# Value products of a head in steps over the next head's jobs, four jobs between scores and transposes, and weight splits in quarters

## The chip, the cores and the metric

The kernel runs on one core of one Trainium2 chip. The metric is the device time of one execution in microseconds (us); lower is better. PE is TensorE (matmuls), DVE is VectorE, ACT is ScalarE, POOL is GpSimd, SP is SyncE, which issues most of the DMAs.

## What is computed

A network of two layers over 512 tokens: 256 context tokens and 256 latent tokens of width 1024. Each layer has a gated feed-forward part, then a mixer, then a second feed-forward part. Only the mixer concerns us. It projects the tokens, runs twelve attention heads and a state-space branch side by side, and puts the joined result through one output projection:

```python
def token_mixers(zx, zc, need_ctx_out, ...):
    a_x = na_attention(rms_norm(heads(qa_x), ...), rms_norm(heads(ka_x), ...), heads(va_x), ka_ch, va_ch, na_rpb)
    kb_c, vb_c = mla_keys_values(ckv_c, kr_c, ...)
    kb_x, vb_x = mla_keys_values(ckv_x, kr_x, ...)
    qb_x = rope_tail(mla_queries(cq_x, ...), row, col)
    kb_x = rope_tail(kb_x, row, col)
    b_x = blocked_joint_attention(qb_x, kb_x, vb_x, kb_c, vb_c, MLA_QK ** -0.5)
    s_x, s_c = s5_mixer(u_x, u_c, need_ctx_out, ...)
    ox = jnp.concatenate([a_x, b_x, s_x], axis=-1)
    if not need_ctx_out:
        return ox, None
    a_c = attend(...)
    b_c = attend(...)
    return ox, jnp.concatenate([a_c, b_c, s_c], axis=-1)
```

Heads 0 to 5 (`a`) are neighbourhood attention with a bias; heads 6 to 11 (`b`) are latent attention, whose queries, keys and values come from an up-projection of a narrow latent vector, with a norm and a rotation. Latent tokens attend to all 512 tokens, context tokens to the 256 context tokens. Context outputs are needed in layer 0 only (`need_ctx_out`). The state-space branch ends in a GELU and a gated linear unit (GLU). Softmax is over the keys, as usual: maximum, exponential, sum, division.

## The kernel before

Each layer's mixer ends in a stage that runs the twelve heads (`attention`). A head is cut into jobs: ("x", h, 0) and ("x", h, 1) for the two 128-row tiles of latent queries against 512 keys, and in layer 0 also ("c", h, 0) for both tiles of context queries, each against 256 keys. Layer 0 has 36 jobs, layer 1 has 24. In the profiled execution layer 0's stage lies at about 578 to 726 us, layer 1's at about 1677 to 1779 us.

The loop over jobs writes the order in which every engine takes its instructions; nothing reorders them at run time. In turn `i` it issues:

- the scores of job `i`: three matmuls on PE (L1522, context L1530; two more for the bias of heads 0 to 5, L1525) into one of four accumulator banks, the maximum on DVE (L1533, tile `m`), the exponential on ACT (L1537, tile `e`, its sum in `su`);
- the keys and queries of coming heads (`after`): copies that ACT and DVE share (L1444, L1445, L1454, L1455; for latent heads L1471, L1472, L1474, L1475);
- the scaling of job `i-1`: reciprocal on DVE (L1542) and a multiplication (L1544), on POOL for the first latent tile and for context, on DVE for the second latent tile;
- the transposes of job `i-LAG`, with LAG = 3: four on PE (L1553), copied out by DVE (L1559) or ACT (L1561) into `PTx` or `PTc`;
- the value products of a pair of heads, two turns after the pair's last transposes: 8 products for the latent rows or 4 for the context rows, in which the two heads take turns (L1571), then ACT and DVE evict both heads at once (L1574, L1575, into `xn`);
- one step of `latent()`: an up-projection for one token tile (L292 to L294), its norm and rotation, later the two halves of the GLU (L1360 to L1363), and at the end the split of the first output weight.

A weight is split into a rounded part and the rest: ACT copies halves (L252), DVE or POOL subtract (L253). PSUM banks: four accumulators (`acc`) for scores, and banks `t` and `b`, handed out by `tp()`, for transposes, value products, up-projections and the GLU. The output projection reads the planes of the mixer's output in the order `ks`. Bias for heads 0 to 5 is prepared on POOL (L1457 to L1460).

## Time and profile before

| | us |
|---|---|
| median of three runs | 2004.27 |
| lowest and highest | 2002.52 and 2012.45 |
| the profiled execution, its own time | 2008.59 |
| the profiled execution, span | 2006.8 |

Over the span PE is busy 95%, DVE 46%, ACT 34%, POOL 33%, and the mean granted clock of PE is 0.98 of full speed. An average over the span hides that the feed-forward parts and the two attention stages are different: the first keep PE busy without a break, the second don't. So the profile is read by stretches: how much of a stretch each engine works, who waits for whom in it, and then the timeline of the engine that waits. A timeline row gives the start, the duration, the engine, the line, the operation with its output and inputs, the count, and in brackets how long the engine stood idle before and what ended that.

### The profile page before, as it was taken

The numbers are of one execution on the slowest core, as the hardware profiler recorded it, in microseconds if no ns is written. First come the engines' busy times: TensorE is split into PE (matmuls) and PEld (weight loads), VectorE is DVE, ScalarE is ACT, GpSimd is POOL, SyncE is SP. The second block draws the span as 40 slices with busy tenths as digits, with TensorE's granted clock in tenths as the row PEclk, the third lists the DMA queues.
The fourth block names the chain that finished last, engine by engine and source line by source line (L and its number), as shares of the span: only waits on it lengthen the run. The fifth ranks groups of instructions, "written<-read, shape, count | busy, mean of one in ns | idle before, by whom it ended". The sixth has DMA issues, their size and how long they took to land. (4 is left out here: it accounts for less than half of the span.)

```text
span 2006.8 us, 28327 instructions
## 1 busy us (share of the span) xinstructions
PE 1904.8 (95%) x11435; PEld 1582.0 (79%) x11435; DVE 914.7 (46%) x1585; ACT 689.8 (34%) x1146; POOL 656.2 (33%) x739
## 2 busy tenths in 40 slices
PE   7999999999887799999999999999999998699999
PEld 4777777788886578788888877777788887579999
DVE  6443233255456545232332454422433645655555
ACT  4421222233345534222222342122122434545433
POOL 2146460134457443100101223845212445641000
PEclk9999999999989899999999999999999988999999
DMA  9655656444412014543322355646523451227653
GB/s 308 178 178 170 211 188 206 136 119 126 156 19 72 22 43 126 170 133 97 100 89 90 114 170 168 201 148 222 174 76 108 146 162 28 83 92 224 189 184 112
DMA packets 364102, 277.77 MB, mean 138 GB/s; under 512 B 29854, under 2 KB 355812, under 8 KB 363972
## 3 DMA queue, kind: packets, MB, share of 16 engines
q1 hardware_dynamic: 361008, 268.44, 43.5%
q0 software_dynamic: 1888, 7.31, 1.0%
q8 instruction: 90, 1.47, 0.3%
q10 hardware_dynamic: 1076, 0.22, 0.1%
...
## 5 line engine op out<-in xcount | busy, mean ns | idle before, releaser
L292 PE MATMUL acc<-xn,spl 128*128 128x512 f32 (+1 forms) x1648 | 591.3, 359 | 2.3 <-DVE xn L571 1.2
L293 PE MATMUL acc<-xn,spl 128*128 128x512 f32 (+1 forms) x1648 | 584.6, 355 | 1.9 <-DVE xn L398 0.2
L294 PE MATMUL acc<-xn,spl 128*128 128x512 f32 (+1 forms) x1648 | 580.9, 353 | 0.2 <-DVE spl L253 0.2
L253 DVE TENSOR_TENSOR spl<-raw,spl 128x1024 fp32r<-128x1024 f32 (+2 forms) x312 | 398.2, 1313 | 278.6 <-ACT spl L252 276.8
L252 ACT ACTIVATE spl<-raw 128x1024 fp32r<-128x1024 f32 (+3 forms) x344 | 324.0, 989 | 321.5 <-PE acc L294 164.9
L674 POOL TENSOR_TENSOR hid<-hv,hid 128x512 fp32r<-128x512 f32 (+1 forms) x88 | 101.8, 1156 | 854.0 <-ACT hid L673 854.0
L292 PEld LDWEIGHTS acc<-xn,spl 128*128 128x128 f32 x1648 | 311.7, 189 | 64.2 <-issue 17.8
L293 PEld LDWEIGHTS acc<-xn,spl 128*128 128x128 f32 x1648 | 311.8, 189 | 46.9 <-DVE xn L572 4.6
L294 PEld LDWEIGHTS acc<-xn,spl 128*128 128x128 f32 x1648 | 311.7, 189 | 44.1 <-DVE spl L253 0.9
L292 PE MATMUL acc<-hid,spl 128*128 128x512 f32 (+1 forms) x740 | 265.2, 358 | 0.0
L293 PE MATMUL acc<-hid,spl 128*128 128x512 f32 (+1 forms) x740 | 262.0, 354 | 0.0
L294 PE MATMUL acc<-hid,spl 128*128 128x512 f32 (+1 forms) x740 | 261.7, 354 | 0.0
L671 DVE TENSOR_TENSOR hv<-sl,acc 128x512 f32<-128x512 f32 (+1 forms) x88 | 54.6, 620 | 362.7 <-PE acc L294 350.7
L673 ACT ACTIVATE hid<-hv 128x512 fp32r<-128x512 f32 (+1 forms) x88 | 50.9, 579 | 383.2 <-DVE hv L671 383.2
L731 DVE SCALAR_TENSOR_TENSOR h<-acc,mod,h 128x256 f32<-128x256 f32 x192 | 84.9, 478 | 207.3 <-PE acc L294 207.3
L292 PEld LDWEIGHTS acc<-hid,spl 128*128 128x128 f32 x740 | 139.8, 189 | 25.2 <-issue 6.4
L294 PEld LDWEIGHTS acc<-hid,spl 128*128 128x128 f32 x740 | 139.9, 189 | 19.6
L293 PEld LDWEIGHTS acc<-hid,spl 128*128 128x128 f32 x740 | 140.0, 189 | 18.6
L293 PE MATMUL acc<-spl,xn 128*128 128x384 f32 (+1 forms) x288 | 98.0, 340 | 8.5 <-DVE spl L253 8.2
L292 PE MATMUL acc<-spl,xn 128*128 128x384 f32 (+1 forms) x288 | 101.2, 351 | 0.0
L294 PE MATMUL acc<-spl,xn 128*128 128x384 f32 (+1 forms) x288 | 97.5, 338 | 0.0
L669 ACT ACTIVATE sl<-acc 128x512 f32<-128x512 f32 (+1 forms) x88 | 47.7, 541 | 133.8 <-PE acc L294 127.5
...
## 6 DMA issues: line engine op xcount, KB each, us to landing
...
```

The source lines that it names most:

```text
L252: nc.scalar.activation(s[:, 0, a:b], raw[:, a:b], AF.Copy)
L253: (nc.gpsimd if mix and b == n else nc.vector).tensor_tensor(s[:, 1, a:b], raw[:, a:b], s[:, 0, a:b].bitcast(F32), op=OP.subtract)
L292: mm(out, sl[0], sr[0], start=start, stop=False)
L293: mm(out, sl[0], sr[1], start=False, stop=False)
L294: mm(out, sl[1], sr[0], start=False, stop=stop)
L669: nc.scalar.activation(sl[:, c], pg[:, c], AF.Silu)
L671: nc.vector.tensor_tensor(hv[:, c], sl[:, c], pu[:, c], op=OP.mult)
L673: nc.scalar.activation(hd[:, 0, c], hv[:, c], AF.Copy)
L674: nc.gpsimd.tensor_tensor(hd[:, 1, c], hv[:, c], hd[:, 0, c].bitcast(F32), op=OP.subtract)
L731: self.nc.vector.scalar_tensor_tensor(self.h[:, n, c], ps[:, c], self.mod[l][:, gate, n, s:s + 1], self.h[:, n, c], op0=OP.mult, op1=OP.add)
```

## The change

- The value products of one head become a generator (`pv`), in steps of one product. Two are issued per turn (`pvs(2)`), beginning one turn after the last transposes of the head, so they are spread over the jobs of the next head. Both heads of a pair share one bank `b`, which `tp()` doesn't hand out any more in this stage. An eviction follows the last product of the odd head, for latent and context rows each.
- LAG is 4; there are five buffers for `e` and `m`, six for `su`, two for `PTx` and `PTc`.
- The up-projections and the GLU take accumulators instead of `tp()` banks.
- The first step of `latent()` is issued before the first keys. The rotation of the shared key part goes one tile at a time into the first four steps.
- Weights are split in quarters (`parts`), one or two per step: ACT copies, DVE and POOL subtract in turn.
- The GLU (both halves in one step) and the split of the first output weight move into a new generator, `readout`, which takes the place of `latent` from job 19 in layer 0 and job 13 in layer 1.
- All scalings run on DVE but those of context rows of heads 6 to 11, which stay on POOL.
- Copies of transposes: DVE takes the second latent tile, ACT all others.
- The output projection reads the planes of heads 0 to 5 first, then the GLU's, then those of the latent heads.

```diff
--- before.py
+++ after.py
@@ -276,6 +276,22 @@
             j += 1
         if j < n:
             self.split(j)
+
+    def parts(self):
+
+        j = self.cur
+        if j in self.spl:
+            return []
+        nc, raw, n = self.nc, self.raws[j], self.width(j)
+        s = self.splp.tile([128, 2, 2048], F32R, name="spl", tag="spl")
+        self.spl[j] = s
+
+        def piece(i):
+            c = slice(i * n // 4, (i + 1) * n // 4)
+            nc.scalar.activation(s[:, 0, c], raw[:, c], AF.Copy)
+            (nc.vector, nc.gpsimd)[i % 2].tensor_tensor(s[:, 1, c], raw[:, c], s[:, 0, c].bitcast(F32), op=OP.subtract)
+
+        return [(lambda i=i: piece(i)) for i in range(4)]
 
     def fillers(self):
         while self.cur < len(self.units) and self.units[self.cur][0] == "mod":
@@ -1294,7 +1310,7 @@
         qs, kn, ss = {}, {}, {}
 
         def upproj(ct, w, nk, n, t):
-            ps = [self.tp(), self.tp()]
+            ps = [self.acc(), self.acc()]
             c = slice(128 * t, 128 * t + 128)
             for hf in range(2):
                 for k in range(nk):
@@ -1353,7 +1369,7 @@
 
             pg = {}
             for m in (2 + n, n):
-                pg[m] = self.tp()
+                pg[m] = self.acc()
                 for k in range(2):
                     self.mm3(pg[m][:, c], (wg[:, 0, k, m * 128:m * 128 + 128], wg[:, 1, k, m * 128:m * 128 + 128]), (yh[:, 0, k, c], yh[:, 1, k, c]), k == 0, k == 1)
             eg = mp2.tile([128, 576], F32, name="sq6")[:, 0:T]
@@ -1364,34 +1380,48 @@
 
         def latent():
 
-            w = self.take("uq", (l,))[:, :, 0:1728].rearrange("p s (k n) -> p s k n", k=3)
-            for t in (2, 3, 0, 1):
-                rope(kr[:, t].unsqueeze(1), t, 1, 1)
+            w = self.take("uq", (l,), False)[:, :, 0:1728].rearrange("p s (k n) -> p s k n", k=3)
+            parts = self.parts()
             seq = [(qhead, qstat, qtail, t) for t in [2, 3] + qt_[:-2]]
             nqs = len(seq)
             seq += [(khead, kstat, ktail, t) for t in al]
             for i in range(len(seq) + 2):
                 if i == nqs:
-                    w = self.take("ukv", (l,), True)[:, :, 0:1536].rearrange("p s (k n) -> p s k n", k=2)
+                    for f in parts:
+                        f()
+                    w = self.take("ukv", (l,), False)[:, :, 0:1536].rearrange("p s (k n) -> p s k n", k=2)
+                    parts = self.parts()
                 if i < len(seq):
                     seq[i][0](seq[i][3], w)
+                if i < 4:
+                    t = (2, 3, 0, 1)[i]
+                    rope(kr[:, t].unsqueeze(1), t, 1, 1)
                 for j in (1, 2):
                     if 0 <= i - j < len(seq):
                         seq[i - j][j](seq[i - j][3])
+                for f in parts[0:(1, 2)[i < nqs and nqs < 4]]:
+                    f()
+                    parts.remove(f)
                 yield
+            for f in parts:
+                f()
+
+        def readout():
             wg = self.take("glu", (l,), False)[:, :, 0:1024].rearrange("p s (k n) -> p s k n", k=2)
             for n in range(2):
                 glu(n, wg)
+            yield
+            for f in self.parts():
+                f()
                 yield
-            self.ahead()
-
-        self.attention(l, need, qt_, qk, nv, qs, kn, mv, biases, bias, xn, mp2, latent())
-
+
+        self.attention(l, need, qt_, qk, nv, qs, kn, mv, biases, bias, xn, mp2, latent(), readout())
         es.close()
+
         self.norm_open()
         self.sq_begin()
         halves = (0, 1) if need else (1,)
-        ks = [6, 7, 3, 4, 5, 0, 1, 2]
+        ks = [0, 1, 2, 6, 7, 3, 4, 5]
         for u in range(4):
             w = (early if u == 3 else self.take("out", (l, u))).rearrange("p s (k n) -> p s k n", k=8)
             ps = [self.acc(), self.acc()]
@@ -1418,7 +1448,7 @@
             for n in (2 * u, 2 * u + 1):
                 self.sq_tile(n, c)
 
-    def attention(self, l, need, qt_, qk, nv, qs, kn, mv, biases, bias, ox, ap, latent):
+    def attention(self, l, need, qt_, qk, nv, qs, kn, mv, biases, bias, ox, ap, latent, readout):
 
 
 
@@ -1529,10 +1559,10 @@
                     for i, (q, k) in enumerate(terms):
                         mm(s[:, 256 * b:256 * b + 256], q[:, 128 * b:128 * b + 128], k[:, 0:256], start=i == 0, stop=i == 2)
                 nb, n = 2, 256
-            m = ap.tile([128, 2], F32, name="m", bufs=4)
+            m = ap.tile([128, 2], F32, name="m", bufs=5)
             V.tensor_reduce(m[:, 0:nb], s.rearrange("p (b n) -> p b n", b=nb), axis=AX, op=OP.max, negate=True)
-            e = ap.tile([128, 512], F32, name="e", bufs=4)
-            su = ap.tile([128, 2], F32, name="su", bufs=4)
+            e = ap.tile([128, 512], F32, name="e", bufs=5)
+            su = ap.tile([128, 2], F32, name="su", bufs=6)
             for i in range(nb):
                 S.activation(e[:, i * n:i * n + n], s[:, i * n:i * n + n], AF.Exp, bias=m[:, i:i + 1], accum_out=su[:, i:i + 1])
             st[j] = (e, su, nb, n)
@@ -1541,13 +1571,13 @@
             e, su, nb, n = st[j]
             V.reciprocal(su[:, 0:nb], su[:, 0:nb])
             for i in range(nb):
-                (P if j[2] == 0 else V).tensor_scalar(e[:, i * n:i * n + n], e[:, i * n:i * n + n], su[:, i:i + 1], None, op0=OP.mult)
+                (P if j[0] == "c" and j[1] >= 6 else V).tensor_scalar(e[:, i * n:i * n + n], e[:, i * n:i * n + n], su[:, i:i + 1], None, op0=OP.mult)
 
         def transposes(j):
             kind, h, t = j
             e = st.pop(j)[0]
             if (kind, h) not in PT:
-                PT[kind, h] = ap.tile([128, 4 if kind == "x" else 2, 256], F32, name=f"PT{kind}", bufs=3)
+                PT[kind, h] = ap.tile([128, 4 if kind == "x" else 2, 256], F32, name=f"PT{kind}", bufs=2)
             p = self.tp()
             for i in range(4):
                 nc.tensor.transpose(p[:, 128 * i:128 * i + 128], e[:, 128 * i:128 * i + 128], self.ident)
@@ -1555,28 +1585,41 @@
                 d, v = PT[kind, h][:, :, 128 * t:128 * t + 128], p.rearrange("p (k q) -> p k q", k=4)
             else:
                 d, v = PT[kind, h].rearrange("p k (t q) -> p t k q", t=2), p.rearrange("p (t k q) -> p t k q", t=2, k=2)
-            if t or (kind == "c" and h % 2):
+            if t:
                 V.tensor_copy(d, v)
             else:
                 S.activation(d, v, AF.Copy)
-            if h % 2 and (t or kind == "c"):
-                pend.append((kind, h))
-
-        def pv(kind, h):
-            o = self.tp()
-            nk = 4 if kind == "x" else 2
-            pts = [PT.pop((kind, h - 1)), PT.pop((kind, h))]
-            for k in range(nk):
-                for i in range(2):
-                    mm(o[64 * i:64 * i + 64, 0:256], value(h - 1 + i)(k), pts[i][:, k, :], start=(k == 0), stop=(k == nk - 1))
-            c = slice(256, 512) if kind == "x" else slice(0, 256)
-            f = h // 2 + 2
-            S.activation(ox[:, 0, f, c], o[:, 0:256], AF.Copy)
-            V.tensor_tensor(ox[:, 1, f, c], o[:, 0:256], ox[:, 0, f, c].bitcast(F32), op=OP.subtract)
-
-        pend = []
-        LAG = 3
-        old = [[], []]
+            if kind == "c" or (t and not need):
+                pend.append(h)
+
+        def pv(h):
+
+            i, f = h % 2, h // 2 + 2
+            if i == 0:
+                outs[h] = self.pm.tile([128, 512], F32, name="b", tag="b")
+            o = outs[h - i]
+            for kind in ("x", "c") if need else ("x",):
+                pt = PT.pop((kind, h))
+                c = slice(256, 512) if kind == "x" else slice(0, 256)
+                nk = 4 if kind == "x" else 2
+                for k in range(nk):
+                    mm(o[64 * i:64 * i + 64, c], value(h)(k), pt[:, k, :], start=k == 0, stop=k == nk - 1)
+                    if i and k == nk - 1:
+                        S.activation(ox[:, 0, f, c], o[:, c], AF.Copy)
+                        V.tensor_tensor(ox[:, 1, f, c], o[:, c], ox[:, 0, f, c].bitcast(F32), op=OP.subtract)
+                    yield
+
+        def pvs(n):
+            while n and steps:
+                if next(steps[0], 0) == 0:
+                    steps.pop(0)
+                else:
+                    n -= 1
+
+        pend, steps, outs = [], [], {}
+        LAG = 4
+        self.bank = True
+        next(latent)
         keys(0)
         queries(0)
         queries(1)
@@ -1588,13 +1631,15 @@
                 scale(jobs[i - 1])
             if i >= LAG:
                 transposes(jobs[i - LAG])
-            for a in old.pop(0):
-                pv(*a)
-            old.append(pend[:])
+            pvs(2)
+            steps += [pv(h) for h in pend]
             pend.clear()
-            next(latent, None)
-        for a in old[0] + old[1]:
-            pv(*a)
+            next(latent if i < 6 * each + 1 else readout, None)
+        while steps:
+            pvs(1)
+        for _ in readout:
+            pass
+        self.bank = None
 
 
     def run(self):
```

On PE, in heads 9 and 10 of layer 0 (L1522, L1530 are scores, L1553 transposes, L1571 value products, a pair in turns; `mv` are the values of latent heads), before:

```order
L1522 MATMUL acc<-xn,qz_4762 128x512 x3
L1553 MATMUL t<-k,e 128x128 x4
L1522 MATMUL acc<-xn,qz_4762 128x512 x3
L1553 MATMUL t<-k,e 128x128 x4
L1530 MATMUL acc<-xn,qz_4762 128x256 x6
L1553 MATMUL t<-k,e 128x128 x4
L1522 MATMUL acc<-kt,qz_4763 128x512 x3
L1553 MATMUL b<-k,e 128x128 x4
L1571 MATMUL t<-PTx,mv 64x256 x8
L1522 MATMUL acc<-kt,qz_4763 128x512 x3
L1553 MATMUL t<-k,e 128x128 x4
L1571 MATMUL t<-PTc,mv 64x256 x4
L1530 MATMUL acc<-kt,qz_4763 128x256 x6
```

and now (L1552, L1560 are scores, L1583 transposes, L1606 value products):

```order
L1552 MATMUL acc<-xn,qz_4762 128x512 x3
L1583 MATMUL t<-k,e 128x128 x4
L1606 MATMUL b<-PTc,mv 64x256 x2
L1552 MATMUL acc<-xn,qz_4762 128x512 x3
L1583 MATMUL t<-k,e 128x128 x4
L1606 MATMUL b<-PTx,mv 64x256 x2
L1560 MATMUL acc<-xn,qz_4762 128x256 x6
L1583 MATMUL t<-k,e 128x128 x4
L1606 MATMUL b<-PTx,mv 64x256 x2
L1552 MATMUL acc<-kt,qz_4763 128x512 x3
L1583 MATMUL t<-k,e 128x128 x4
L1606 MATMUL b<-PTc,mv 64x256 x2
```

The two bursts of 8 and 4 are now groups of two behind the transposes of each job.

On DVE, in jobs 11 to 14 of layer 0, around the GLU (L1361, L1363) and the split (L253), before:

```order
L1575 TENSOR_TENSOR xn<-t,xn 128x256
L1361 SCALAR_TENSOR_TENSOR sq_5381<-b,smT_90,sq_5381 128x512
L1363 TENSOR_TENSOR xn<-sq_5381,xn 128x512
L1533 TENSOR_REDUCE m<-acc 128x2
L1455 TENSOR_TENSOR qz_4763<-t,qz_4763 64x512
L1542 RECIPROCAL su<-su 128x1
L1544 TENSOR_SCALAR e<-e,su 128x512
L1361 SCALAR_TENSOR_TENSOR sq_5434<-b,smT_90,sq_5434 128x512
L1533 TENSOR_REDUCE m<-acc 128x1
L1542 RECIPROCAL su<-su 128x2
L253 TENSOR_TENSOR spl<-raw,spl 128x1024
L1533 TENSOR_REDUCE m<-acc 128x1
```

and now, around job 20 (L1377, L1379 are the GLU, L1563 the maximum, L1574 the scale, L292 a quarter of the split):

```order
L1572 RECIPROCAL su<-su 128x1
L1574 TENSOR_SCALAR e<-e,su 128x512
L1377 SCALAR_TENSOR_TENSOR sq_5624<-acc,smT_90,sq_5624 128x512
L1379 TENSOR_TENSOR xn<-sq_5624,xn 128x512
L1377 SCALAR_TENSOR_TENSOR sq_5643<-acc,smT_90,sq_5643 128x512
L1563 TENSOR_REDUCE m<-acc 128x2
L1502 TENSOR_TENSOR qz_4762<-t,qz_4762 96x512
L1505 SCALAR_TENSOR_TENSOR xn<-t,kg_92,xn 96x512
L1572 RECIPROCAL su<-su 128x1
L1574 TENSOR_SCALAR e<-e,su 128x512
L1589 COPY PTx<-t 128x4x128
L292 TENSOR_TENSOR spl<-raw,spl 128x512
```

The GLU's operations stood one job apart, each ahead of a maximum; now three stand together, eight jobs later, and the split has smaller pieces.

On DVE, in a late pair of heads of layer 0 (L1575 evictions, L1533 maxima, L1559 copies of transposes), before:

```order
L1544 TENSOR_SCALAR e<-e,su 128x512
L1559 COPY PTc<-t 128x2x2x128
L1533 TENSOR_REDUCE m<-acc 128x1
L1542 RECIPROCAL su<-su 128x2
L1575 TENSOR_TENSOR xn<-t,xn 128x256
L1533 TENSOR_REDUCE m<-acc 128x1
L1542 RECIPROCAL su<-su 128x1
L1559 COPY PTx<-b 128x4x128
L1575 TENSOR_TENSOR xn<-t,xn 128x256
L1533 TENSOR_REDUCE m<-acc 128x2
L1472 TENSOR_TENSOR qz_4763<-t,qz_4763 96x512
```

and now (L1609 evictions, L1589 copies):

```order
L1572 RECIPROCAL su<-su 128x1
L1574 TENSOR_SCALAR e<-e,su 128x512
L1589 COPY PTx<-t 128x4x128
L1609 TENSOR_TENSOR xn<-b,xn 128x256
L1563 TENSOR_REDUCE m<-acc 128x1
L1572 RECIPROCAL su<-su 128x2
L1609 TENSOR_TENSOR xn<-b,xn 128x256
L1563 TENSOR_REDUCE m<-acc 128x1
L1572 RECIPROCAL su<-su 128x1
L1574 TENSOR_SCALAR e<-e,su 128x512
L1563 TENSOR_REDUCE m<-acc 128x2
```

Copies of context transposes have left DVE, scales of the first latent tile have come to it.

## Rows read from the trace of the kernel before

**Rows 1.** Busy time by stretch: length; busy (count) PE, PEld, DVE, ACT, POOL; clock, DMA.

```profile
586.90:629.70 42.80, 35.90 (x210) 33.96 (x211) 28.57 (x60) 20.02 (x53) 35.12 (x49) 0.87 0.38 87
629.70:675.30 45.60, 31.69 (x185) 23.18 (x185) 23.67 (x51) 26.41 (x55) 22.93 (x22) 0.89 0.12 41
675.30:725.50 50.20, 42.38 (x275) 31.45 (x275) 30.80 (x70) 26.33 (x73) 22.15 (x20) 0.90 0.00 1
1684.80:1717.50 32.70, 26.64 (x151) 24.30 (x150) 21.45 (x45) 15.43 (x40) 26.28 (x42) 0.92 0.46 91
1717.50:1743.90 26.40, 16.28 (x94) 13.11 (x95) 15.42 (x33) 16.52 (x29) 16.28 (x16) 0.88 0.17 58
1743.90:1779.30 35.40, 29.68 (x200) 20.50 (x199) 25.00 (x57) 19.39 (x48) 11.21 (x7) 0.99 0.10 31
639.71:642.56 2.85, 2.85 (x13) 2.36 (x13) 1.52 (x4) 1.12 (x1) 2.17 (x3) 1.00 0.00 0
```

**Rows 2.** Waits, 578 to 726: who waited, for whom; total us, times, longest.

```profile
DVE xn L1575 <- ACT xn L1574: 16.3, 9, 5.4
...
PE t L1553 <- DVE e L1544: 7.3, 4, 2.6
...
PE t L1553 <- POOL e L1544: 6.6, 6, 2.9
...
PE t L292 <- DVE xn L1445: 2.9, 1, 2.9
```

**Rows 3.** Timeline of DVE, 641 to 668: start, duration, what, [idle before].

```profile
643.46 0.75 DVE L1361 SCALAR_TENSOR_TENSOR sq<-b,smT,sq 128x512 f32<-128x512 f32 x1 [2.23 <-PE acc L1530]
...
645.52 0.68 DVE L1533 TENSOR_REDUCE m<-acc 128x2 f32<-128x512 f32 x1
...
655.50 1.22 DVE L253 TENSOR_TENSOR spl<-raw,spl 128x1024 fp32r<-128x1024 f32 x1 [3.55 <-ACT spl L252]
...
665.88 0.42 DVE L1575 TENSOR_TENSOR xn<-t,xn 128x256 fp32r<-128x256 f32 x1 [5.41 <-ACT xn L1574]
```

**Rows 4.** Timeline of PE, value products of layer 1, short windows.

```profile
1746.11 0.44 PE L1571 MATMUL t<-PTx,nv 128*64 128x256 f32 x2 [0.98 <-DVE qz L1472]
...
1746.11 1.30 PE L1571 MATMUL t<-PTx,nv 128*64 128x256 f32 x10 [0.98 <-DVE qz L1472]
...
1776.49 0.43 PE L1571 MATMUL b<-PTx,mv 128*64 128x256 f32 x1
...
1776.49 0.65 PE L1571 MATMUL b<-PTx,mv 128*64 128x256 f32 x2
```

**Rows 5.** Timeline of PE, middle of layer 0.

```profile
660.69 1.11 PE L1553 MATMUL b<-k,e 128*128 128x128 f32 x4 [3.65 <-POOL e L1544]
```

**Rows 6.** Timeline of DVE, 680 to 698, one pair of late heads.

```profile
681.25 0.49 DVE L1544 TENSOR_SCALAR e<-e,su 128x512 f32<-128x512 f32 x1
...
681.65 0.68 DVE L1559 COPY PTc<-t 128x512 f32<-128x512 f32 x1
...
682.25 0.68 DVE L1533 TENSOR_REDUCE m<-acc 128x1 f32<-128x512 f32 x1
...
684.59 0.42 DVE L1575 TENSOR_TENSOR xn<-t,xn 128x256 fp32r<-128x256 f32 x1 [1.59 <-ACT xn L1574]
...
689.38 0.69 DVE L1472 TENSOR_TENSOR qz<-t,qz 96x512 fp32r<-96x512 f32 x1 [1.56 <-ACT qz L1471]
...
697.18 0.49 DVE L1544 TENSOR_SCALAR e<-e,su 128x512 f32<-128x512 f32 x1
```

**Rows 7.** Timeline of DVE, layer 1, split and two late scales.

```profile
1739.60 1.23 DVE L253 TENSOR_TENSOR spl<-raw,spl 128x1024 fp32r<-128x1024 f32 x1 [3.13 <-ACT spl L252]
...
1747.72 0.48 DVE L1544 TENSOR_SCALAR e<-e,su 128x512 f32<-128x512 f32 x1
...
1757.89 0.49 DVE L1544 TENSOR_SCALAR e<-e,su 128x512 f32<-128x512 f32 x1
```

**Rows 8.** Line L1544 on DVE in layer 1: ns least, median, most.

```profile
L1544 DVE TENSOR_SCALAR e<-e,su x12: 485/487/1082, 1697.4 to 1774.5; 128x512 f32<-128x512 f32 x12
```

## Prediction

> **What bounds the kernel now.** The view of busy time by stretch comes first [rows 1]. Everything outside the two attention stages is untouched by the diff, so only these stretches matter: in layer 0 the first eight jobs (586.9 to 629.7), ten jobs in the middle (629.7 to 675.3) and the rest (675.3 to 725.5), and the same three parts of layer 1. PE is the fullest engine in each, but it works 31.69 of 45.60 us in the middle of layer 0 and 16.28 of 26.40 us in the middle of layer 1. No other engine is full there either (DVE 23.67, ACT 26.41 of 45.60), so these middles are made of waits from one in-order queue to another. The view of waits [rows 2] says which: DVE stands 16.3 us for the ACT half of the evictions of finished heads, PE stands 7.3 us for DVE's and 6.6 us for POOL's scaling of the exponentials, and once 2.9 us for a free bank before an up-projection. The timelines show how one stall passes on. PE waits 3.65 us for a scaled tile from POOL before four transposes [rows 5]; the eviction behind that stands in DVE's queue ahead of the next maximum, and DVE is idle for 5.41 us [rows 3]. The half split of the output weight holds DVE for 3.55 us, one half of the GLU for 2.23 us [rows 3].
>
> **The middle of layer 0, jobs 8 to 17.** I walk DVE's queue in its new order and charge start-to-start distances, which lie about 0.08 below the durations. Ten maxima at 0.60 are 6.0; ten reciprocals at 0.18 are 1.8; seven scales of 512 columns at 0.40 (681.25 to 681.65 in [rows 6]) are 2.8; six half scales, which DVE doesn't do before, lie between half of that and all of it, and at 0.30 are 1.8; four copies of transposes at 0.60 [rows 6] are 2.4; seven query and key products at about 0.63 are 4.4; three evictions at 0.35 and one norm product at 0.5 are 1.6. Together 20.8. What stays are four waits for ACT's copy of the queries, which queue behind the exponential, at 1.5 (1.56 in [rows 6]), 6.0, and I leave 1.0 for evictions. DVE's walk gives 27.8.
>
> PE has a walk of its own. Without the GLU, which leaves this stretch, 2 x 2.85 [rows 1] goes from 31.69: 26.0. But the value products get dearer. Today the two heads of a pair go through the two halves of the array in turn: ten records last 1.30, two last 0.44, so each further two take 0.215. At the very end one head goes alone: one record lasts 0.43, two last 0.65, so each takes 0.22 [rows 4]. The new generator issues only one head's products in a row, so a pair's 24 records in layer 0 take 24 x 0.216 = 5.2 instead of 2.6, and 16 in layer 1 take 3.5 instead of 1.7. In the middle, 20 products of two records (8.6) stand where two pairs (5.2) stood; the 3.4 more is 3.9 at the granted clock of 0.89. PE's walk gives 29.9, later than DVE's. I take it: 45.6 - 29.9, **a gain of 15.7**. The Trainium skill, TensorEngine Tiling (Array Packing), section Key Properties, says that tiles of the array operate independently and can run matmuls in parallel. The rows for pairs agree with it, and it speaks against this change; its "up to 2x" would give nothing else than the 0.216 above.
>
> **What is given back.** The GLU stands later as one block in DVE's queue. The first of its halves now holds DVE from 641.2 to the maximum at 645.52, 4.3 [rows 3]; with PE's 2.85 for the second behind it, 7.2 (ends: 4.3, if the second is hidden, and 8.6, twice the first). The quarter splits move behind it too. The half split costs 3.55 + 1.22 = 4.8 [rows 3]; two quarters of the four are DVE's and ACT copies all four. Between nothing and 4.8 I take 2.5. Moved work is still work: layer 0 gives back 9.7.
>
> **First jobs of layer 0.** The wait of 2.9 for a bank [rows 2] goes, since up-projections take from the four accumulators and one of them is put ahead. Against it stand rotations and split pieces that go ahead of the bias on POOL, which is busy 35.12 of 42.80 [rows 1]. I take a gain of 2.4; ends 0 and 2.9.
>
> **Last jobs of layer 0.** A pair of heads takes 15.93 today (681.25 to 697.18, the same scale of the next pair, [rows 6]). The new queue has two more scales (+0.80), no context copy (-0.60), and one eviction wait left (1.5 for 1.59 + 0.5): 15.75. PE's busy time of 42.38 grows by three pairs, 3 x 2.6 / 0.90 = 8.7, to 51.1 of 50.2, with the tails of its pipeline counted in it. So both queues end together, and I take a gain of 0.5 in these jobs and a loss of 0.5 at the end, where eight products of one head follow the last transposes alone (16 x 0.216 = 3.5) instead of twelve in pairs (24 x 0.108 = 2.6): nothing in sum.
>
> **Layer 1.** Five jobs now take 26.4 [rows 1], while later ones go at 10.17 for four (1747.72 to 1757.89, [rows 7]), 12.7 for five. With the moved scales and the queries of the next head I put 14.4; a gain of 12.0, of which 0.2 is lost at the start (pieces on POOL). Back come the GLU at half the columns, 0.6 x 7.2 = 4.3, and the splits: the half split holds DVE 3.13 + 1.23 [rows 7], between 0 and 4.4 I take 2.0. In the late jobs each head's second tile is now scaled on DVE instead of POOL, 0.4 x 5.5 heads = 2.2. Layer 1 gains 12.0 - 0.2 - 4.3 - 2.0 - 2.2 = 3.3. The values' extra 1.7 / 0.99 per pair lies beside DVE's queue there: PE works 29.68 of 35.40.
>
> **Sum.** -15.7 + 9.7 - 2.4 = -8.4 in layer 0, -3.3 in layer 1: -11.7. The profiled execution took 2008.59 (2006.8 of it the span), 4.3 above the median; the difference is taken from the median: 2004.27 - 11.7 = **1992.6**.
>
> **The rivals.**
> *The stall only moves.* The GLU costs its far end in both layers (+1.4 and +0.8), the splits theirs (+2.3 and +2.4), the start gains nothing (+2.4): -11.7 + 9.3 = -2.4, **2002**. For it: in-order queues, and a block of four GLU operations ahead of a maximum. Against: the maxima are four jobs ahead of the transposes, so PE has something to do.
>
> *More waits go than I count.* I keep the eviction waits of the late jobs, but spread products could be finished long before DVE asks. Of 16.3 us, 5.41 are counted above; the other 10.9 [rows 2] would give **1982**. For it: the eviction is asked for once per pair, and its products end one job earlier. Against: ACT's own queue holds the copy behind exponentials.
>
> *The doubled value products land on PE's path, slower than before.* Six pairs cost 15.6 more in layer 0 and 10.4 in layer 1, at granted clocks of 0.90 and 0.95 28.2; 3.9 of it is in the sum. If all of the other 24.3 lands: **2017**. It beats the gain of 11.7 as soon as half of it lands. For it: the late part of layer 0 comes out full on PE. Against: layer 1 has 5.7 us of room in 35.4, and transposes no longer wait for POOL in these stretches.
>
> *DVE and POOL get in each other's way, slower too.* All 24 x scales of a layer and six heads' context halves now run on DVE. The twelve of layer 1 last 485 ns at least, 487 in the median and 1082 at worst [rows 8]; the excess is 0.6. If 36 of the 60 on DVE are long, 21.6 come on top: **2014**. Below 20 of 60 the change still gains. Against: most are at 487, while POOL is busy in four fifths of the first jobs. The Trainium skill, SBUF — State Buffer, section Who interferes with whom, says that DVE's tensor_scalar in its two-port modes and a GpSimd instruction exclude each other for a whole instruction. The maximum of 1082 fits it; by that rule alone the scales moved from POOL would also stretch what stays on POOL.
>
> **How the numbers follow.** Forecast (1986 to 1999) 0.36, stall only moves 0.24, more waits go 0.20, doubled values 0.13, port 0.07. The bound of 0.5%, about what a measurement of this kernel can tell from no change, is 10.0 us: 1994.2 and 2014.3. Two thirds of the forecast and all of the larger gain are faster, 0.44; a third of it and the moved stall are the same, 0.36; the other two are slower or close to it, 0.20. The range leaves a tenth at each side: 1976 to 2014.
>
> **What the profile after would show.** Right: the ten middle jobs of layer 0 in about 30 us without waits of PE over 2 us; the waits of DVE for evictions at a third; the GLU as one hole of 7 us in DVE's maxima; late pairs of heads at 15.8 in layer 0 and 11 in layer 1; value records of one head 0.216 apart. Wrong: PE without gaps in the late jobs while a pair takes over 17 (doubled values); scales of 1 us in rows (port); a pair below 14.5 (waits that I kept are gone). The forecast falls with the price of the GLU first, then with the values.

## The result and the profile after

The changed kernel takes 2035.64 us in the median (2031.41 to 2037.42) where the kernel before took 2005.63 beside it: 1.0142 times as long, 95% interval 1.0110 to 1.0173. The prediction was 1992.6 with a range of 1976 to 2014. It was wrong, in the direction and in the range.

The view of busy time by stretch, after, cut at the same jobs as [rows 1] (jobs 0, 8, 18 and 27 of layer 0; 0, 6, 11 and 18 of layer 1). Columns as in [rows 1]:

```profile
587.80:634.40 46.60, 37.30 (x207) 32.47 (x206) 28.75 (x70) 20.31 (x56) 28.46 (x41) 0.89 0.31 65
634.40:666.60 32.20, 24.95 (x133) 16.90 (x133) 21.63 (x49) 16.36 (x44) 7.27 (x9) 0.95 0.09 31
666.60:706.50 39.90, 33.77 (x161) 22.34 (x162) 21.40 (x45) 21.92 (x49) 7.65 (x7) 0.91 0.08 27
706.50:738.40 31.90, 28.27 (x150) 17.43 (x150) 15.52 (x37) 14.98 (x40) 7.56 (x8) 1.00 0.00 1
1700.80:1734.70 33.90, 25.09 (x123) 21.09 (x123) 21.90 (x52) 14.72 (x41) 23.95 (x38) 0.85 0.37 67
1734.70:1753.70 19.00, 16.62 (x75) 11.40 (x74) 11.93 (x26) 7.79 (x19) 7.34 (x9) 0.83 0.25 88
1753.70:1784.60 30.90, 25.07 (x125) 16.80 (x123) 19.83 (x42) 17.36 (x37) 2.44 (x3) 0.89 0.00 1
1784.60:1807.80 23.20, 21.73 (x106) 12.95 (x106) 13.09 (x30) 8.88 (x21) 0.82 (x1) 1.00 0.13 46
```

Timed from the maxima of DVE, in us, with the kernel before beside it. "End" runs from the last maximum to the first matmul of the output projection:

| | jobs 0-8 | 8-18 | 18-27 | 27-35 | end | stage |
|---|---|---|---|---|---|---|
| layer 0, before | 42.9 | 45.6 | 22.9 | 20.3 | 7.0 | 138.6 |
| layer 0, after | 46.6 | 32.3 | 39.8 | 20.2 | 11.7 | 150.6 |

| | jobs 0-6 | 6-11 | 11-18 | 18-23 | end | stage |
|---|---|---|---|---|---|---|
| layer 1, before | 32.7 | 26.3 | 18.6 | 10.3 | 6.5 | 94.5 |
| layer 1, after | 33.9 | 19.0 | 30.9 | 13.2 | 10.0 | 107.0 |

The two stages together are 24.5 us longer. The middles did shrink, by 13.3 and 7.3. The jobs behind them grew by 16.9 and 12.3, and both ends grew. Between the stages nothing changes but the order of planes. This part takes 956 to 960 us in the profiled runs with the old order and 957 to 963 with the new, so a single profile says nothing of a few us there.

The new rows on PE, against [rows 4 and 5]. First the waits of layer 0 (who, for whom: total, times, longest), then the timeline of PE in late jobs and at the end of layer 0:

```profile
PE b L1606 <- DVE xn L1609: 9.3, 9, 2.5
...
PE acc L309 <- POOL spl L292: 5.0, 1, 5.0
```

```profile
694.82 1.97 PE L1606 MATMUL b<-PTc,nv 128*64 128x256 f32 x4 [2.47 <-DVE xn L1609]
...
718.65 0.97 PE L1560 MATMUL acc<-xn,qz 96*128 96x256 f32 x6
...
719.45 0.60 PE L1583 MATMUL t<-k,e 128*128 128x128 f32 x4
...
719.99 1.08 PE L1606 MATMUL b<-PTx,mv 128*64 128x256 f32 x4
...
720.99 0.97 PE L1552 MATMUL acc<-kt,qz 96*128 96x512 f32 x3
...
737.37 1.08 PE L1606 MATMUL b<-PTc,mv 128*64 128x256 f32 x4 [0.93 <-DVE xn L1609]
```

Where nothing is waited for, a turn goes from 718.65 (scores) over 719.45 (transposes) and 719.99 (four records of one head) to 720.99, the next scores: 0.80 + 0.54 + 1.00 = 2.34 us, without a gap on PE. Nearly half of it is value products, at 0.25 a record with the change of shape counted in; within the group they lie 0.216 apart, as predicted. In this turn PE is the bound. Even so the last jobs of layer 0 (27 to 35) did not get longer, 20.2 us against 20.3. Their stretches, first after, then before:

```profile
706.50:726.70 20.20, 18.44 (x99) 12.19 (x100) 11.64 (x29) 11.12 (x30) 5.73 (x6) 1.00 0.00 1
```

```profile
698.20:718.50 20.30, 17.73 (x108) 13.11 (x105) 12.19 (x30) 10.80 (x30) 10.14 (x9) 0.83 0.00 1
```

PE works more of the stretch than before, and its granted clock is 1.00 where it was 0.83.

The wait at 694.82 has a second price: after 2.47 us of standing PE's four records took 1.97 instead of 1.08. The granted clock was 1.00 from 688.0 to 692.3 and 0.50, the lower of its two levels (1.2 of 2.4 GHz), from 694.8 to 700.0:

```profile
694.80:697.00 2.20, 2.18 (x5) 1.03 (x6) 0.64 (x2) 1.44 (x4) 1.39 (x2) 0.50 0.91 317
```

The wait itself is new: the context products of an odd head stand behind the eviction of its latent rows, because both lie in the one bank `b`.

The late GLU in the timeline of DVE, layer 0, against [rows 3]:

```profile
673.55 0.75 DVE L1377 SCALAR_TENSOR_TENSOR sq<-acc,smT,sq 128x512 f32<-128x512 f32 x1 [3.02 <-PE acc L310]
...
675.00 0.69 DVE L1379 TENSOR_TENSOR xn<-sq,xn 128x512 fp32r<-128x512 f32 x1 [0.70 <-ACT xn L1378]
...
676.50 0.75 DVE L1377 SCALAR_TENSOR_TENSOR sq<-acc,smT,sq 128x512 f32<-128x512 f32 x1 [0.82 <-ACT sq L1376]
...
677.17 0.68 DVE L1563 TENSOR_REDUCE m<-acc 128x2 f32<-128x512 f32 x1
...
680.76 0.69 DVE L1502 TENSOR_TENSOR qz<-t,qz 96x512 fp32r<-96x512 f32 x1 [2.91 <-ACT qz L1501]
```

From the scale ahead (its end is 3.02 before 673.55) to the maximum at 677.17 it is one hole of 6.6 us, and 2.91 more before 680.76, since ACT does the second half's rounding and a table load ahead of the exponential.

### The profile page after: what moved, and what is told of

It reads as the page before. It is cut to its first block, busy times and chain, and to the rows that moved or that the text cites. A ratio compares the mean times of both kernels' runs of the same rounds, so it can differ in the third digit from the quotient of the medians.

```text
span 2035.3 us, 28306 instructions
## 1 busy us (share of the span) xinstructions
PE 1936.6 (95%) x11435; PEld 1590.4 (78%) x11435; DVE 926.2 (46%) x1619; ACT 690.1 (34%) x1160; POOL 612.5 (30%) x711
## 3 DMA queue, kind: packets, MB, share of 16 engines
q1 hardware_dynamic: 361008, 268.44, 42.9%
## 4 chain that ended last, share of the span: by engine, by line
PE 56%; DVE 8%; ACT 4%; POOL 2%; DMA 1%; issue 1%; SPq 0%; ACTq 0%; DVEq 0%; POOLq 0%
PE acc L308 17%; PE acc L309 16%; PE acc L310 16%; PE b L1606 2%; PE b L485 1%; ACT e L1567 1%; PE acc L1552 1%; DVE m L1563 1%; DVE xm L580 1%; DVE xn L590 1%; DVE e L1574 1%; PE t L1583 1%; DVE xn L588 0%; ACT spl L252 0%; POOL sqs L541 0%
## 5 line engine op out<-in xcount | busy, mean ns | idle before, releaser
L253 DVE TENSOR_TENSOR spl<-raw,spl 128x1024 fp32r<-128x1024 f32 (+3 forms) x304 | 392.1, 1327 | 269.5 <-ACT spl L252 267.7
L252 ACT ACTIVATE spl<-raw 128x1024 fp32r<-128x1024 f32 (+3 forms) x332 | 314.6, 995 | 321.0 <-PE acc L310 160.7
L309 PEld LDWEIGHTS acc<-hid,spl 128*128 128x128 f32 x740 | 140.0, 189 | 18.6
L309 PE MATMUL acc<-spl,xn 128*128 128x384 f32 (+1 forms) x356 | 120.9, 340 | 14.8 <-DVE spl L253 8.2
L308 PE MATMUL acc<-spl,xn 128*128 128x384 f32 (+1 forms) x356 | 125.3, 352 | 3.4 <-ACT e L1567 3.2
L310 PE MATMUL acc<-spl,xn 128*128 128x384 f32 (+1 forms) x356 | 120.3, 338 | 0.0
```

The source lines that it names most:

```text
L252: nc.scalar.activation(s[:, 0, a:b], raw[:, a:b], AF.Copy)
L253: (nc.gpsimd if mix and b == n else nc.vector).tensor_tensor(s[:, 1, a:b], raw[:, a:b], s[:, 0, a:b].bitcast(F32), op=OP.subtract)
L308: mm(out, sl[0], sr[0], start=start, stop=False)
L309: mm(out, sl[0], sr[1], start=False, stop=False)
L310: mm(out, sl[1], sr[0], start=False, stop=stop)
```

## The experiments

Each kernel ran beside the kernel before on the same chip; a ratio is to that, with its 95% interval. Four theories were to be told apart: (A) the products of one head at a time fill PE; (B) the late GLU block costs more there; (C) the waits for evictions in the shared bank; (D) the splits in quarters. A fifth (E) came out of their results.

**Half of the products.**

```diff
-                    mm(o[64 * i:64 * i + 64, c], value(h)(k), pt[:, k, :], ..., stop=k == nk - 1)
+                    if k % 2 == 0:
+                        mm(o[64 * i:64 * i + 64, c], value(h)(k), pt[:, k, :], ..., stop=k == nk - 2)
```

> The changed kernel with every second value product of a head left out (the output is then not the attention's), steps and evictions in their places. Theory A, the value products of one head at a time fill PE's queue: layer 0 has 72 products of 0.432, layer 1 has 48, half of them is 15.6 + 10.4 = 26 us of PE; where PE is the bound nearly all of it comes back, so 2035.6 - 18 to 26 = 2010 to 2018. Theory B, the loss is the GLU block and the waits of products for evictions and copies: those stay, so less than 8 us come back, 2028 or more.

2023.2, ratio 1.0088 (1.0070 to 1.0106): about 11 us came back, between both theories. PE's waits for evictions stayed (10.5 us in layer 0), so this is the price of the records themselves. It doesn't lie where it was thought to be: jobs 18 to 27 of layer 0 did not fall (41.3 against 39.8); the ends and the late jobs did.

**Evictions behind all products of a head.**

```diff
-                    if i and k == nk - 1:
-                        S.activation(ox[:, 0, f, c], o[:, c], AF.Copy)
...
+                    if i and kind == ("c" if need else "x") and k == nk - 1:
+                        for c in (slice(256, 512), slice(0, 256))[0:2 if need else 1]:
+                            S.activation(ox[:, 0, f, c], o[:, c], AF.Copy)
```

> The changed kernel with the evictions of an odd head issued after all of its products, context ones too, so that no context product stands behind the eviction of the latent rows in the same bank. Theory C, that wait (PE for DVE's eviction, 9.3 us in nine places of layer 0) is lost time: 2035.6 - 6 to 9 = 2027 to 2030, layer 1 unchanged, and the wait of PE for evictions under 3 us. Theory A: PE fills the gap with nothing, but DVE then stands behind two evictions, so the gain is under 3 us.

2040.4, ratio 1.0165 (1.0150 to 1.0181): not better, rather worse. But the edit did not take the wait away. Two evictions now stand one behind the other, and the first products of the next pair wait for both; PE stands longer for evictions in layer 0 than the 9.3 us of the changed kernel:

```profile
PE b L1606 <- DVE xn L1610: 11.5, 5, 3.1
```

So this run does not test theory C. The eviction wait comes back in the pairs below.

**The GLU in its early place.**

```diff
+            wg = self.take("glu", (l,), False)[:, :, 0:1024].rearrange("p s (k n) -> p s k n", k=2)
+            for n in range(2):
+                glu(n, wg)
+                yield
+            for f in self.parts():
...
         def readout():
-            wg = self.take("glu", (l,), False)[:, :, 0:1024].rearrange("p s (k n) -> p s k n", k=2)
...
```

> The changed kernel with the GLU and the split of the output weight put back behind the latent steps (two GLU steps, then a quarter per step, jobs 10 to 15 of layer 0 and 8 to 13 of layer 1). Theory B, the late block of the GLU costs more than in its early place because the late jobs have the longer exchange between DVE and ACT: 6 to 12 us come back, 2024 to 2030. Theory A: PE is as full there as here, the block only moves, within 4 us of 2035.6; there are four more table loads, up to 5 us the other way.

2031.0, ratio 1.0117 (1.0100 to 1.0135), 5 us back by the medians, though the intervals overlap. The stretches moved against each other: jobs 8 to 18 of layer 0 from 32.3 to 41.1, 18 to 27 from 39.8 to 28.8. So the short middle of the changed kernel was, to 9 of its 13 us, only the absence of the GLU.

**Products of both heads in turns, still in steps.**

```diff
+            o = self.pm.tile([128, 512], F32, name="b", tag="b")
+            for kind in ("c", "x") if need else ("x",):
+                pts = [PT.pop((kind, h - 1)), PT.pop((kind, h))]
...
+                    for i in range(2):
+                        mm(o[64 * i:64 * i + 64, c], value(h - 1 + i)(k), pts[i][:, k, :], ...)
...
-            pvs(2)
+            pvs(4)
```

> The changed kernel with the value products of both heads of a pair in turns again, still in steps into the one bank: four products per turn behind the transposes, context rows first, three buffers for the transposed latent rows; the rest as in the changed kernel. Theory A: 26 us of PE come back as in the run with half of the products, less what bursts cost, 2012 to 2022, with a burst of eight records in about 1.1 us. Theory B: under 6 us, 2030 or more.

2020.5, ratio 1.0060 (1.0043 to 1.0077): about 16 us came back. Eight records of a pair take what four of one head take; a row of PE's timeline in this run, and its wait for evictions in layer 0:

```profile
705.60 1.08 PE L1605 MATMUL b<-PTx,mv 128*64 128x256 f32 x8
```

```profile
PE b L1605 <- DVE xn L1608: 0.9, 1, 0.9
```

So the edit takes two things away, the doubled records and nearly all of the 9.3 us of waits for evictions. The 16 us are their joint price; the 11 us of e1_half_products are the records alone. How much the rest owes to the waits (theory C) no run shows by itself.

**Splits in halves, alone and with pairs.**

```diff
-            w = self.take("uq", (l,), False)[:, :, 0:1728]...
-            parts = self.parts()
+            w = self.take("uq", (l,))[:, :, 0:1728]...
...
-                for f in parts[0:(1, 2)[i < nqs and nqs < 4]]:
...
-            for f in self.parts():
-                f()
-                yield
+            self.ahead()
+            yield
```

> The changed kernel with the weight splits undone to two halves ahead of their use, as before (all three places; the output weight's after the GLU). Theory D, the quarters cost: PE waits 5.0 us in layer 0 for the last quarter of the key weight on POOL, and the four jobs behind the GLU of layer 1 take 17.6 us instead of 10.4. The first eight jobs of layer 0 then fall from 46.6 to about 42, the jobs behind the GLU by 2 to 4 in each layer: 2035.6 - 8 to 12 = 2024 to 2028. Rival, a half at once holds DVE's queue for 3 to 5 us as it did before, and what is won at the first place is lost at the other: within 3 us of 2035.6.

> The products in pairs as in the run e4_pairs (2020.5) and the splits in halves. If the two losses are separate places, this is 2020.5 - 8 to 12 = 2008 to 2013, and the same gain as that of halves alone. If PE's full queue was what made the quarters late, the gain is under 4 us: 2016 to 2021.

Alone 2032.9, ratio 1.0127 (1.0108 to 1.0146); with pairs 2023.2, 1.0082 (1.0060 to 1.0104). The first eight jobs of layer 0 fell from 46.6 to 43.0, and with pairs from 46.3 to 43.2, as theory D says. That is the one place that it explains. In the changed kernel PE's timeline shows the wait there, and POOL's what it waited for:

```profile
606.26 0.69 PE L309 MATMUL acc<-spl,xn 128*128 128x384 f32 x1 [5.04 <-POOL spl L292]
```

```profile
605.22 0.99 POOL L292 TENSOR_TENSOR spl<-raw,spl 128x384 fp32r<-128x384 f32 x1
```

The last quarter of the key weight stands behind the rotations of a query tile on POOL and ends when PE has stood for 5 us. Behind the GLU the halves did little (jobs 18 to 27 at 37.6 against 39.8, layer 1 unchanged), and of the total 3 us are seen alone, within the intervals, and nothing with pairs. So the 2 to 4 us that were expected behind the GLU in each layer were seen in layer 0 only.

**Three jobs between scores and transposes, with pairs; then three and five without.**

```diff
-        LAG = 4
+        LAG = 3
```

> The products in pairs as in e4_pairs, with three jobs between scores and transposes instead of four. If the fourth job hides anything, PE waits for DVE's or POOL's scaled tiles in the middle again, and the ten middle jobs of layer 0 (28.9 us in e4_pairs) grow by 3 or more: 2024 to 2030. If it hides nothing once the scales are on DVE, within 3 us of 2020.5.

> The changed kernel with three jobs between scores and transposes, all else as changed. Theory E, four put the DVE copy of the second tile's transposes into the same turn as the copies of the next head's queries and keys, so one turn of DVE is long and the next waits for PE; with three they stand in different turns: 6 to 8 us come back as they did with pairs (2020.5 to 2011.9): 2027 to 2030, over half of it in layer 1. Rival, with pairs it was the burst of four products that collided with the fourth job, without pairs nothing is gained: 2033 to 2038.

> The changed kernel with five jobs between scores and transposes and one more buffer each for maxima, sums and exponentials. Theory E (which turn the copies fall in): with five they stand apart again as with three, so layer 1's late jobs are as fast as with three and the time is 2026 to 2032, with a tail 2 us longer in each layer. Rival, distance as such costs (a longer tail, later value products): five is worse than four, 2038 to 2044.

With pairs and three: 2011.9, ratio 1.0024 (1.0011 to 1.0037). Three alone: 2020.9, 1.0063 (1.0043 to 1.0082). Five (LAG = 5, one more buffer each for `e`, `m`, `su`): 2022.9, 1.0082 (1.0059 to 1.0106). So four, not distance as such, is the bad value: three and five are 16 and 12 us better. Too few buffers are not the reason: five with its one more buffer has no more of them to spare than four. Part of the reason shows in DVE's timeline of one late head of layer 1, first in the changed kernel, then with three:

```profile
1786.71 0.69 DVE L1563 TENSOR_REDUCE m<-acc 128x1 f32<-128x512 f32 x1 [0.87 <-PE acc L1552]
...
1788.52 0.42 DVE L1502 TENSOR_TENSOR qz<-t,qz 96x256 fp32r<-96x256 f32 x1 [1.11 <-ACT qz L1501]
...
1789.09 0.75 DVE L1505 SCALAR_TENSOR_TENSOR kt<-t,kg,kt 96x512 fp32r<-96x512 f32 x1 [0.16 <-ACT kt L1504]
...
1790.35 0.68 DVE L1589 COPY PTx<-t 128x512 f32<-128x512 f32 x1
...
1790.95 0.68 DVE L1563 TENSOR_REDUCE m<-acc 128x1 f32<-128x512 f32 x1
...
1793.10 0.69 DVE L1563 TENSOR_REDUCE m<-acc 128x1 f32<-128x512 f32 x1 [0.88 <-PE acc L1552]
```

```profile
1767.19 0.68 DVE L1563 TENSOR_REDUCE m<-acc 128x1 f32<-128x512 f32 x1
...
1768.99 0.42 DVE L1502 TENSOR_TENSOR qz<-t,qz 96x256 fp32r<-96x256 f32 x1 [1.11 <-ACT qz L1501]
...
1769.56 0.75 DVE L1505 SCALAR_TENSOR_TENSOR xn<-t,kg,xn 96x512 fp32r<-96x512 f32 x1 [0.16 <-ACT xn L1504]
...
1770.82 0.68 DVE L1563 TENSOR_REDUCE m<-acc 128x1 f32<-128x512 f32 x1
...
1772.24 0.68 DVE L1589 COPY PTx<-t 128x512 f32<-128x512 f32 x1
...
1772.85 0.67 DVE L1563 TENSOR_REDUCE m<-acc 128x1 f32<-128x512 f32 x1
```

With four, the copies of the next head's queries (L1502) and keys (L1505) and the copy of the transposes (L1589) stand in one turn, 4.24 us from maximum to maximum (1786.71 to 1790.95), and in the next turn DVE waits 0.88 for PE. With three, L1589 stands in the other turn: 3.63 and 2.03. A head takes 6.39 with four and 5.66 with three. Layer 1's stretches show the second part, the same jobs with four, three and five (11 to 18, then 18 to 23):

```profile
1753.70:1784.60 30.90, 25.07 (x125) 16.80 (x123) 19.83 (x42) 17.36 (x37) 2.44 (x3) 0.89 0.00 1
1784.60:1797.80 13.20, 12.12 (x59) 7.76 (x60) 8.90 (x22) 6.52 (x16) 0.82 (x1) 1.00 0.23 81
```

```profile
1744.00:1770.80 26.80, 23.80 (x127) 15.63 (x127) 18.50 (x40) 17.73 (x38) 2.35 (x3) 1.00 0.00 1
1770.80:1783.10 12.30, 11.56 (x57) 7.23 (x56) 9.52 (x23) 5.98 (x15) 1.24 (x1) 1.00 0.27 87
```

```profile
1742.80:1769.20 26.40, 23.70 (x127) 15.31 (x125) 18.26 (x40) 17.45 (x37) 2.38 (x3) 1.00 0.00 1
1769.20:1781.50 12.30, 11.70 (x58) 7.19 (x57) 9.92 (x24) 6.31 (x16) 1.21 (x1) 1.00 0.27 87
```

In the late jobs the granted clock is 1.00 in all three, and four costs 0.9 over five jobs. In the jobs behind the GLU it is 0.89 with four and 1.00 with three and five, and four costs 4.1 to 4.5. There PE stands 5.8 us with four and 3.0 with three (length less busy time), and works 1.3 longer for about as many records. The longest of these waits, in PE's timeline of the changed kernel, is for the very copy that stands behind the others:

```profile
1776.42 1.97 PE L1606 MATMUL b<-PTx,nv 128*64 128x256 f32 x4 [2.20 <-DVE PTx L1589]
```

The granted clock was 1.00 from 1770.0 to 1774.2 and 0.50 from 1776.4 to 1782.0.

In layer 0 a head has three jobs, and there too four puts L1589 behind L1502 and L1505 in one turn (709.70 to 714.87), while three doesn't. But in the undisturbed late jobs of layer 0 this costs little: jobs 27 to 35 take 20.2 with four, 19.9 with three, 19.6 with five. Behind the GLU of layer 0 they are 39.8, 35.7 and 33.8 for nine jobs, with PE's waits for evictions at 4.2, 1.9 and 0.9 us. So theory E is shown for the late jobs and for this one wait. For the rest of the 12 to 16 us it is argued, since the waits for evictions, the late block and the clock change along with it.

**Scales on POOL again, with pairs.**

```diff
-                (P if j[0] == "c" and j[1] >= 6 else V).tensor_scalar(e[...], ...)
+                (P if j[2] == 0 else V).tensor_scalar(e[...], ...)
```

> The products in pairs as in e4_pairs, with the scales of first latent tiles and of all context jobs on POOL again. If moving them to DVE was right, PE or the transposes wait for POOL's 1.6 us tiles again: 2023 to 2030. If DVE's queue is what the late jobs go by, 0.4 us a head come back in the late jobs of both layers, 2014 to 2018.

2017.9, ratio 1.0054 (1.0035 to 1.0073), against 1.0060 with the scales on DVE: no difference to speak of in either direction.

**The three losses undone together, with and without the late GLU.** The diffs are those above.

> Products in pairs, three jobs, splits in halves. If the three losses are separate places, e7_pairs_lag3 (2011.9) less the 3 to 5 us that halves give in the first eight jobs of layer 0: 2007 to 2009, level with the kernel before. If halves do nothing for the total, 2011 to 2014.

> The same with the GLU back in its early place too; what is left of the change is the steps, the banks, the scales on DVE and the order of planes. If the late GLU costs 3 to 5 us here as it did alone (2035.6 to 2031.0), 2003 to 2006, under the kernel before. If its stall only moves, 2007 to 2012.

2008.8, ratio 1.0008 (0.9994 to 1.0021): level with the kernel before. So these three parts together make up the loss, and the forecast gain doesn't appear without them either. The order of planes, which stayed, was never undone by itself. With the early GLU 2015.0, 1.0042 (1.0025 to 1.0058): here the late place is the better one by 6 us, the other way round than e3_glu_early seemed to say. What the GLU costs depends on what stands around it.

**Bursts in what was left.** The products of a pair as in the kernel before (`pv(kind, h)`, two turns late), with three jobs and halves:

```diff
-            pvs(2)
-            steps += [pv(h) for h in pend]
+            for a in old.pop(0):
+                pv(*a)
+            old.append(pend[:])
```

> The changed kernel with three jobs, splits in halves, and the value products of a pair in bursts of 8 and 4, two turns late, as before; banks for transposes handed out four at a time again. What is left of the change: the scales, the late GLU, the banks of the up-projections, the order of planes. Against e11_pairs_lag3_halves (2008.8) it shows what steps of a pair are worth. If steps help, the middle of layer 0 grows from 31.7 by 3 or more, 2012 to 2016. If they are worth nothing, 2005 to 2011.

2010.9, ratio 1.0016 (1.0001 to 1.0030), against 1.0008 with pairs in steps. Spreading the products is worth nothing that can be measured here.

**Single parts put into the kernel before: scales, GLU, both, one head at a time.**

```diff
-                (P if j[2] == 0 else V).tensor_scalar(e[...], ...)
+                (P if j[0] == "c" and j[1] >= 6 else V).tensor_scalar(e[...], ...)
```

```diff
+        def readout():
+            wg = self.take("glu", (l,), False)[...]
+            for n in range(2):
+                glu(n, wg)
+            yield
+            self.ahead()
+            yield
...
-            next(latent, None)
+            next(latent if i < 6 * each + 1 else readout, None)
```

> The kernel before with one edit: all scales on DVE but those of context rows of heads 6 to 11. If POOL's scales were the cause of the waits in the middle, the ten middle jobs of layer 0 fall by 4 to 8 from 45.6 and the late jobs of layer 1 rise by 2: 1998 to 2004. If the scales only move the wait, 2004 to 2011.

> The kernel before with one edit: the GLU in one block at job 19 of layer 0 and job 13 of layer 1, the split of the output weight behind it in halves. If the block costs less than the two halves in the early place, with two table loads less in each layer, 2000 to 2004. If it costs the same there as here, the middle falls by 12 to 15 and the jobs behind it rise by as much: 2004 to 2011.

> The kernel before with both of these edits. If they add up, the sum of the two differences; a version under 2000 would beat both kernels. If the stall moves again, 2003 to 2010.

Scales alone: 2013.2, ratio 1.0031 (1.0017 to 1.0044), slower. GLU alone: 2004.7, 0.9986 (0.9971 to 1.0001). Both: 2007.0, 0.9996 (0.9982 to 1.0010). The stretches settle where the middle's gain came from. First the run with the GLU alone (jobs 8-18 and 18-27 of layer 0, 6-11 and 11-18 of layer 1), then the run with the scales alone (jobs 8-18 of layer 0):

```profile
628.90:660.70 31.80, 23.71 (x161) 17.15 (x161) 20.64 (x47) 16.56 (x45) 19.10 (x20) 1.00 0.07 25
660.70:692.80 32.10, 26.79 (x157) 20.19 (x157) 18.83 (x40) 20.27 (x44) 14.77 (x11) 0.89 0.10 33
1709.40:1727.50 18.10, 12.61 (x67) 10.47 (x68) 12.20 (x29) 7.73 (x19) 12.99 (x14) 0.81 0.24 85
1727.50:1754.50 27.00, 20.52 (x133) 15.28 (x132) 16.46 (x35) 17.66 (x36) 7.88 (x5) 0.94 0.12 39
```

```profile
627.40:672.70 45.30, 33.30 (x171) 24.63 (x169) 29.55 (x59) 26.22 (x55) 12.80 (x13) 0.81 0.08 26
```

Moving the GLU and the output weight's split alone takes the ten middle jobs from 45.6 to 31.8, all that the whole change took there. Moving the scales alone leaves them at 45.3.

> The kernel before with one edit: the value products of one head at a time in steps of two per job into the one bank, three jobs between scores and transposes as before. PE gets 15.6 + 10.4 = 26 us more to do. If what was lost there is what pairs gave back (8 us with three jobs, 15 with four), 2014 to 2024, with the late jobs of both layers longer and the tails 2 to 3 longer. If steps remove stalls as the prediction had it, 2000 to 2008.

```diff
+        self.bank = True
...
-            for a in old.pop(0):
-                pv(*a)
-            old.append(pend[:])
+            pvs(2)
+            steps += [pv(h) for h in pend]
```

2023.5, ratio 1.0082 (1.0063 to 1.0101): 16 us slower, the same size as what pairs gave back to the changed kernel. It has the wait for the eviction and the end of the changed kernel, too; from PE's timeline:

```profile
706.49 1.08 PE L1576 MATMUL b<-PTx,mv 128*64 128x256 f32 x4 [0.86 <-DVE xn L1579]
...
726.97 1.08 PE L1576 MATMUL b<-PTc,mv 128*64 128x256 f32 x4 [0.93 <-DVE xn L1579]
```

Layer 0's end is 10.1 and layer 1's 8.3 against 7.0 and 6.5, and jobs 18 to 27 of layer 0 take 27.8 against 22.9.

**The late GLU and the banks.** `upproj` and `glu` take `self.acc()` for `self.tp()`, on top of e15_before_glu.

> The kernel before with the late GLU (e15_before_glu, 2004.7) and the up-projections and the GLU in the four accumulator banks. PE waited 2.9 and 2.5 us for a transpose bank before an up-projection or the GLU in layer 0; if these go, 1998 to 2003. If scores then wait for the accumulators instead, 2003 to 2009.

2003.3 over twelve runs, ratio 0.9979 (0.9967 to 0.9991): the one version of the eighteen in this study that is faster than the kernel before by more than its interval, by about 4 us. Against e15_before_glu (0.9986) the banks alone show nothing that is clear of noise.

## Why the prediction was wrong

The forecast was a gain of 11.7 us, and the kernel lost 30. Undoing two parts of the change, the products of one head at a time and the distance of four, brings 24 us back (e7_pairs_lag3); with halves in place of quarters the kernel is level with the kernel before (e11_pairs_lag3_halves). So two steps failed most: the prediction put the doubled products at nothing outside the middle of layer 0, and it had no price for the distance. What is left to explain, a gain that isn't there, is work that moved.

**The middle (forecast 15.7, measured 13.3).** The size came out near, by luck; the reason didn't. I read the middle's waits as waits for POOL's scales, evictions and banks and walked the queues without the GLU; e15_before_glu and e14_before_scale show that the GLU and the split, with what they make wait, are worth 13.8 by themselves and the scales next to nothing. The waits of [rows 2] and [rows 5] were how their delay passed from queue to queue, not causes of their own. Taking them away leaves time that something else fills. One term was right: the doubled products were put at 3.4 here, and pairs bring the middle from 32.3 to 28.9.

**The middle of layer 1 (forecast 12.0, measured 7.3).** Here the size failed as well. The price of 14.4 for five jobs came from later jobs of the kernel before; the jobs took 19.0. With the GLU alone moved they took 18.1, and the jobs behind them 27.0 instead of 18.6 (e15_before_glu): 8.2 won and 8.4 given back, where the prediction had 12.0 and 6.3. So layer 1 had nothing to win from the move.

**Given back (9.7 in layer 0).** For the GLU and halves alone this was right: e15_before_glu has 32.1 against 22.9, 9.2. In the changed kernel it is 16.9, because the block falls into jobs that are slower by the next two points.

**Doubled value products.** The 0.216 a record was right, and so were the rival's 26 us of added work on PE. The step that failed is "lies beside DVE's queue there" for layer 1 and "both queues end together" for layer 0. In layer 1 I compared PE's sum with the whole stretch (29.68 of 35.40) and saw room. In jobs 18 to 23 there was less, 8.10 of 10.30 before; after, PE works 12.12 of 13.20 there, and DVE stands for scores that are issued behind the products, 2.8 us against 0.3 before and 0.9 with pairs:

```profile
1762.40:1772.70 10.30, 8.10 (x54) 5.62 (x53) 8.61 (x21) 5.86 (x15) 4.69 (x3) 1.00 0.01 3
```

```profile
DVE m L1563 <- PE acc L1552: 2.8, 3, 1.1
```

In layer 0 my own sum had PE at 51.1 of 50.2, and I still booked a gain of 0.5. (The pair of heads beside it was added up wrongly, too: the terms give 15.54, not 15.75.) From job 27 to 35 it did come out even, at the higher clock; the end and the jobs behind the GLU did not, where pairs give back 2.5 and 3.7. The records alone cost 11 us (e1_half_products), with the waits for evictions in the shared bank 16 (e4_pairs, and e17_steps_alone the other way). The rival that said so had 0.13 and ended at 2017, with the forecast gain counted in; most of the rest of the way to 2035.6 is that the gain isn't there and the next point.

**Four jobs between scores and transposes.** The prediction has no price for it; it counted the distance as a help ("PE has something to do"). It costs 12 to 16 us against three and five. The help is real in one place: with pairs the middle of layer 0 takes 28.9 with four and 31.5 with three. What is lost behind it and in layer 1 is more. It puts all of DVE's copies into one turn, which could be seen in the order of the program before the run; that this accounts for all of the cost is not shown. The two losses overlap: pairs give 0.8% and three jobs 0.8%, both together 1.2%.

**First jobs of layer 0 (forecast -2.4, measured +3.7).** The bank wait did go, but that is worth nothing: with the accumulators in the kernel before these jobs take 42.9 (e18_before_glu_acc), without them 42.8 (e15_before_glu), and PE stands elsewhere. The quarters cost 3.6, for POOL's last quarter. I had put 0.5 for pieces on POOL although it was busy for four fifths of that stretch.

**Ends (forecast +0.5 in layer 0 and nothing in layer 1, measured +4.7 and +3.5).** What follows the last transposes alone was counted, what waits in steps there (0.93 for an eviction at 737.37, products of earlier heads that are still due) was not. Pairs give back 2.5 and 1.6.

**The port.** The rival was right that DVE and POOL get in each other's way, but its price of 21.6 was far too high. In the changed kernel POOL's quarter of the split starts 0.04 us ahead of DVE's scale (DVE's row is shown first):

```profile
692.33 1.50 DVE L1574 TENSOR_SCALAR e<-e,su 128x512 f32<-128x512 f32 x1
```

```profile
692.29 1.26 POOL L292 TENSOR_TENSOR spl<-raw,spl 128x512 fp32r<-128x512 f32 x1 [4.24 <-ACT spl L291]
```

The scale takes 1.50 instead of 0.49 and ends 0.28 after POOL's row; one at 1774.51 takes 1.25 and ends 0.27 after POOL's. The Trainium skill, SBUF — State Buffer, section Who interferes with whom, says that a tensor_scalar in DVE's two-port modes and a GpSimd instruction exclude each other for a whole instruction; these rows agree. Such rows are few: the median is 0.486 in layer 0 and 0.487 in layer 1, and of the 48 scales of 512 columns on DVE seven are longer than 0.6, by 4.2 us in sum. But these two stand in DVE's queue right ahead of the eviction and the copy for which PE waited 2.47 us (694.82) and 2.20 us (1776.42), and behind both waits the granted clock was 0.50. e8_pairs_pool shows no gain from putting the scales back; moved alone into the kernel before they cost 6 us (e14_before_scale), how much of it by the port is not shown.

The range failed with the forecast: each rival was priced alone, the doubled products and a stall that moves came together, and the distance of four was in none of them.
